# A split-precision decoder step on one core: float32 side work on every second unit, part of the weight splitting on GpSimd, a finer start and a spread convolution

## The chip, the core and the metric

The kernel runs on one core of one Trainium2 chip. The metric is the device time of one execution in microseconds (us). The kernel before takes 1319.54 us, the median of three runs that lie between 1318.51 and 1319.89.

The engines are named as the profile names them: PE is the matrix engine (PEld its weight loads), DVE the vector engine, ACT the scalar engine, POOL is GpSimd, SP the sync engine, which here only issues transfers. Each engine runs its own instructions strictly in the order in which the program issued them, and waits at an instruction until what it needs has been signalled.

## The reference, cut to what matters

One step of a one-layer decoder, in float32, for 256 prompt tokens and 8 x 8 sample tokens (320 columns in all) at a width of 2048:

```python
z = rmsnorm(x, g_mix) @ w_in                    # 2048 x 3584
b, c, hc, q, k, v, qx = jnp.split(z, IN_SPLITS, axis=-1)
# three head groups, side by side
y_conv = b * short_conv(c * hc, conv_w)         # width 512, 3 taps, 2 rows of history
y_swa  = sink_attention(q, k, v, rel_bias, ...) # 8 q heads, 2 kv heads, window 128
y_x    = cross_attention(qx, mk, mv)            # 4 heads, 256 memory tokens (w_mem_k, w_mem_v)
x = x + concat([y_conv, y_swa, y_x]) @ w_out
x = x + square(relu(rmsnorm(x, g_mlp) @ w_up)) @ w_down   # 2048 x 8192 and back
```

q, k and qx are normalized per head. Besides y, the new caches are returned (keys, values, memory keys and values, and the last rows of the convolution's input).

## The kernel before

**Tiling.** Activations are kept transposed, 128 channels by 320 columns per k-tile. All weights are float32. They come in 360 *pieces* of 256 rows by 512 columns (512 KB each), loaded by SP into four `raw` buffers. Each piece is split in two: ACT copies it to `wh`, rounded to the matrix engine's fast float32 format, and DVE forms `wl = raw - wh`, the rest (`split_piece`, L407). Activations are split the same way into S0h and S0l or S1h and S1l. A product is then three fast matmuls: wh by the high part, wh by the low part, wl by the high part. So there are 8256 main matmuls of 320 columns and 192 of 512 columns (those of the memory keys and values).

**Order of the work.** The pieces are taken in groups of 512 output columns: first seven groups of w_in with the two memory groups between (cross-attention q, then k and v, memory k, memory v, q, q, c, h, b), then w_out, then w_up and w_down in turns. A *unit* is 12 main matmuls (6 in the memory groups). The whole instruction order is written out by a planner while the program is built: `run_unit` (L469) issues a unit, `boundary` (L461) then steps the side jobs through `Side.step` (L218). A side job (norms, attention, bias, convolution) is a generator that issues some instructions, then yields for so many units. `after(tiles)` (L272) makes a job yield until a model of the engines' clocks (`Pace`, L98) says that the tiles are ready; `bank()` (L276) makes it yield until one of four PSUM banks is free. `side.until` (L237) steps jobs without issuing matmuls until named flags are up. What the planner writes is an order; waits on the chip happen where its model was wrong.

**The side work on PE.** Between units the jobs place *side visits*: transposes and attention scores in plain float32, others in the fast format, and the sample attention in column-tiled matmuls (32 output rows each). In the trace main matmuls write `mm` and all side visits write `ax`.

**Splitting.** `split_piece` for piece i+4 can start once piece i's unit is done. The function `rest` in it (L426) issues the subtraction on DVE and after it the load of the next piece on SP. POOL issues small transfers (table of the relative bias, the one-hot matrix c_hot, sinks, selector, g_k_x), six 128x512 memsets, and outputs.

**The convolution.** `h_evac` (L1124), called for each of four 128-row blocks m when its h is done, makes u = c*h, and at once the three taps: one `tensor_scalar` and two `scalar_tensor_tensor` on DVE over 336 columns. `b_evac` (L1153) multiplies by b.

**The start.** SP loads two k-tiles of x, the first piece in two halves, two more k-tiles of x, piece 1, four k-tiles of x in two loads, piece 2, and so on. ACT's queue loads the small columns table and the identity. Nine matmuls on ones keep PE busy until the first data land. In the first 48 main matmuls, the first two pieces go m pair by m pair: all matmuls of a piece for two blocks m, then for the other two.

**Lines to follow.** Nearly all instructions are recorded at one helper line, L166 (in the changed file L169), so groups are told apart by tile names.

Of the kernel before, what the change touches and what calls it, by code (L numbers as in the profile page):

```python
# [34 lines left out]
LAG = 6.0  # L35
WARM = 9
# [56 lines left out]
class Pace:  # L93
# [12 lines left out]
    def cost(self, eng, op, out, ins):  # L106
        n = max(a.free_size() for a in [out] + ins)
        if eng == "pe":
            n = out.free_size()
            if ins[0].dtype == F32R:  # L110
                return 0.0033 + n / 2400.0
            quarter = 0.25 if out.partition_size() == 32 else 1.0
            return 0.0009 * n if op == "transpose" else max(0.11, n / 600.0) * quarter
        if eng == "act":
            return 0.1 + n * 0.00083
        if eng == "dve":
            return 0.08 + n * 0.00104
# [17 lines left out]
    def load(self, out):  # L135
        start = max(self.clock["dma"], self.clock["pe"])
        self.clock["dma"] = start + out.free_size() * 4 * out.partition_size() / 330e3
        self.wrote[out.name] = (self.clock["dma"] + (2.0 if out.name.startswith("raw") else LAG), "dma")

# [7 lines left out]
class Paced:  # L147
# [3 lines left out]
    def __getattr__(self, op):  # L151
# [4 lines left out]
        def issue(*args, **kw):  # L156
            aps = [a for a in list(kw.values()) + list(args) if isinstance(a, bass.AP)]
            out = kw["out"] if "out" in kw else args[0]
            if op == "dma_start":
                if out.name not in self.pace.dram:  # L160
                    self.pace.load(out)
            else:
                if "accum_out" in kw:
                    self.pace.wrote[kw["accum_out"].name] = (self.pace.clock[self.name] + 0.5, self.name)
                self.pace.issue(self.name, op, out, [a for a in aps if a is not out])
            return f(*args, **kw)  # L166
# [81 lines left out]
def trunk_step(ctx: ExitStack, tc: tile.TileContext, I, O):  # L248
# [27 lines left out]
    def bank():  # L276
        return ax.need([P, 512])
# [20 lines left out]
    act.dma_start(out=ident, in_=I["c_ident"])  # L298
# [24 lines left out]
    rm = const.tile([P, 2], F32, name="rm")  # L323

# [71 lines left out]
    def load_piece():  # L396
# [3 lines left out]
        count["load"] += 1  # L400
        w, k0, c0 = pieces[i]
        t = raw_p.tile([P, 2, 512], F32, name="raw", tag="raw")
        for c in [slice(0, 2)] if i else [slice(0, 1), slice(1, 2)]:
            sp.dma_start(out=t[:, c, :], in_=w[c0 // 512, k0 // 2][:, c, :])
        wt[i] = t

    def split_piece():  # L407
# [9 lines left out]
        if not i:  # L417
            for c in range(2):
                side.until([f"x0{c}"])
                act.activation(out=h[:, c, :], in_=r[:, c, :], func=AF.Copy)  # L420
                dve.tensor_tensor(out=l[:, c, :], in0=r[:, c, :], in1=h[:, c, :].bitcast(F32), op=ALU.subtract)
            load_piece()
# [9 lines left out]
    def add_group(w, c0, korder, a, evac, kind="std", needs=None, pre=None, k0=0):  # L432
# [6 lines left out]
        if kind == "std":  # L439
            ends = [[([m], [i, i + 1]) for m in range(4)] for i in (0, n - 2)]  # L440
            if not base:
                ends[0] = [([2 * q, 2 * q + 1], [i]) for i in range(2) for q in range(2)]
# [26 lines left out]
    def run_unit(un):  # L469
# [10 lines left out]
        if un["kind"] == "std":  # L480
# [40 lines left out]
    def load_x(b, cuts=((0, 4),)):  # L521
        t = lx.must([P, 4, T])
        for lo, hi in cuts:
            sp.dma_start(out=t[:, lo:hi, :], in_=I["xT"][:, 4 * b + lo:4 * b + hi, :])
        xblk[b] = t
# [10 lines left out]
    def x_job():  # L536
        for i in range(8):
            for k in (2 * i, 2 * i + 1):
                split_act(S0h[:, k, :], S0l[:, k, :], xblk[k // 4][:, k % 4, :], gcol("g_mix", k))
                if not i:  # L540
                    side.flags.add(f"x0{k}")
                    yield 1
# [6 lines left out]
    def mean_rsqrt(out, sq):  # L549

        yield from after(sq)
        bk = yield from bank()
# [59 lines left out]
    def start_head(name, ps, gain, dest):  # L612
# [9 lines left out]
        def gen():  # L622
# [13 lines left out]
            bk = yield from bank()  # L636
# [146 lines left out]
    def cross_prompt(h):  # L783
# [4 lines left out]
        bk = yield from bank()  # L788
# [25 lines left out]
        bk = yield from bank()  # L814
# [24 lines left out]
    def cross_sample(f):  # L839
# [34 lines left out]
        for kb in range(2):  # L874
            t = yield from half()
            pool.memset(t, 0.0)
# [13 lines left out]
        for b in range(4):  # L890
            cur = queue.pop(0)
            yield from after(*cur)
            for kb in range(2):
# [38 lines left out]
    def swa_prompt(g, hp):  # L932
# [7 lines left out]
        for blk in range(2):  # L940
# [20 lines left out]
            yield 1  # L961
            pt = yield from half()
            act.activation(out=pt[:, 0:2 * nk], in_=bk[:, 0:2 * nk], func=AF.Copy)
            ax.put(bk)
            w2.put(s)
# [147 lines left out]
    def conv_pre_job():  # L1113
        st["u"] = yield from lx.need([P, 4, UC])
        cc = yield from half()
        pool.memset(st["u"][:, :, 0:2], 0.0)
# [250 lines left out]
```

## Time and profile before

| | us |
|---|---|
| median of three runs | 1319.54 |
| the profiled execution's own time | 1319.31 |
| its span (first to last instruction) | 1316.8 |
| what lies around the span | 2.5 |
| PE busy | 1309.4 (99%) |
| DVE busy | 675.2 (51%) |
| ACT busy | 540.5 (41%) |
| POOL busy | 17.7 (1%), 36 instructions |

The page counts PE as busy from the first modelled start of a matmul to its modelled end, so matmuls that follow each other overlap in it: one main matmul of 320 columns has a mean of 310 ns, while 12 of them in a row take 1.76 us in the chain of waits. So the pace is read from the chain, and durations of DVE, ACT and POOL instructions from the groups. A wait of PE is listed with the engine, or the transfer, whose signal ended it.

### The profile page before, as it was taken

To read this page: it belongs to the slowest core of one execution; us is meant where nothing else is said; L and a number is where in the kernel's file an instruction comes from. 1 tells how busy PE (TensorE), PEld (TensorE's weight loads), DVE (VectorE), ACT (ScalarE), POOL (GpSimd) and SP (SyncE) were. 2 spreads that over 40 slices of the span, in tenths; PEclk is the share of its full clock that TensorE was granted. 3 is DMA by queue.
4 is the path that set the end of the run, shared out by engine and by line. 5 is a ranking of instruction groups with operands and counts; after the bars stand their busy time and mean duration, and the time that the engine had idled before them with its cause. 6 is when DMAs were issued, how large, how long until landed. Compare 5 with 4: busy or idle time off the path is not lost.

```text
span 1316.8 us, 21550 instructions
## 1 busy us (share of the span) xinstructions
PE 1309.4 (99%) x8954; PEld 1286.9 (98%) x8954; DVE 675.2 (51%) x1022; ACT 540.5 (41%) x801; POOL 17.7 (1%) x36
## 2 busy tenths in 40 slices
PE   9999999999999999999999999999999999999998
PEld 8988999999999999999999999999999999999998
DVE  6876666776576444444344444344443344444342
ACT  7784554343355344332244432234442324433321
POOL 1011000000000000000000000000000000000000
PEclk9999999999999999999999999999999999999999
DMA  8667545366344444444444444444444444444552
GB/s 310 240 200 267 189 165 200 109 220 250 128 145 161 145 152 136 160 147 158 146 155 133 152 159 154 147 157 129 160 154 152 153 151 128 161 154 152 176 167 72
DMA packets 65025, 217.03 MB, mean 165 GB/s; under 512 B 8374, under 2 KB 10142, under 8 KB 64897
## 3 DMA queue, kind: packets, MB, share of 16 engines
q1 hardware_dynamic: 62896, 210.38, 47.8%
q0 software_dynamic: 1744, 5.19, 1.1%
q8 instruction: 70, 1.15, 0.4%
q14 instruction: 27, 0.21, 0.0%
q10 hardware_dynamic: 288, 0.10, 0.0%
HBM read 211.53 MB, written 7.65 MB: 166 GB/s over the span
## 4 chain that ended last, share of the span: by engine, by line
PE 98%; DMA 1%; DVE 0%; SPq 0%; ACT 0%; issue 0%; POOL 0%; DVEq 0%
PE mm L166 95%; PE ax L166 3%; DMA raw<-in_w_in 0%; DMA w<-in_c_hot 0%; DVE wl L166 0%; SPq L166 0%; ACT wh L166 0%; POOL z L166 0%; DVE lx L166 0%; DVE S0l L166 0%; DVEq L166 0%; DVE z L166 0%
## 5 line engine op out<-in xcount | busy, mean ns | idle before, releaser
L166 DVE TENSOR_TENSOR wl<-raw,wh 128x1024 fp32r<-128x1024 f32 (+1 forms) x361 | 435.9, 1220 | 479.8 <-ACT wh L166 473.2
L166 ACT ACTIVATE wh<-raw 128x1024 fp32r<-128x1024 f32 (+1 forms) x361 | 374.1, 1052 | 629.5 <-PE mm L166 591.0
L166 PE MATMUL mm<-S0h,wh 128*128 128x320 f32 x1472 | 458.1, 311 | 0.4 <-ACT wh L166 0.4
L166 PE MATMUL mm<-S0h,wl 128*128 128x320 f32 x1472 | 455.3, 309 | 1.6 <-DVE wl L166 1.6
L166 PE MATMUL mm<-S0l,wh 128*128 128x320 f32 x1472 | 454.8, 309 | 0.0
L166 PE MATMUL mm<-S1h,wh 128*128 128x320 f32 x1280 | 397.3, 310 | 0.0
L166 PE MATMUL mm<-S1h,wl 128*128 128x320 f32 x1280 | 395.5, 309 | 0.0
L166 PE MATMUL mm<-S1l,wh 128*128 128x320 f32 x1280 | 395.5, 309 | 0.0
L166 PEld LDWEIGHTS mm<-S0h,wh 128*128 128x128 f32 x1472 | 276.4, 188 | 3.8 <-issue 2.7
L166 PEld LDWEIGHTS mm<-S0h,wl 128*128 128x128 f32 x1472 | 276.3, 188 | 2.6 <-DVE wl L166 2.6
L166 PEld LDWEIGHTS mm<-S0l,wh 128*128 128x128 f32 x1472 | 276.5, 188 | 0.1
L166 PEld LDWEIGHTS mm<-S1h,wh 128*128 128x128 f32 x1280 | 240.3, 188 | 0.7 <-issue 0.6
L166 PEld LDWEIGHTS mm<-S1l,wh 128*128 128x128 f32 x1280 | 240.3, 188 | 0.1
L166 PEld LDWEIGHTS mm<-S1h,wl 128*128 128x128 f32 x1280 | 240.2, 188 | 0.0
L166 DVE TENSOR_TENSOR lx<-mm,lx 128x320 f32<-128x320 f32 x96 | 46.9, 489 | 78.7 <-PE mm L166 78.6
L166 ACT ACTIVATE z<-z 128x320 f32<-128x320 f32 (+1 forms) x118 | 54.9, 469 | 65.3 <-DVE z L166 64.2
L166 DVE TENSOR_TENSOR S1l<-z,S1h 128x320 fp32r<-128x320 f32 x68 | 33.4, 491 | 51.8 <-ACT S1h L166 51.8
L166 ACT ACTIVATE S1h<-z 128x320 fp32r<-128x320 f32 x68 | 32.1, 471 | 8.1 <-DVE z L166 6.1
L166 DVE SCALAR_TENSOR_TENSOR z<-mm,r2b 128x320 f32<-128x320 f32 x64 | 31.0, 484 | 0.0
L166 PE MATMUL mm<-wh,S1h 128*128 128x512 f32 x64 | 25.6, 400 | 0.0
L166 PE MATMUL mm<-wh,S1l 128*128 128x512 f32 x64 | 25.1, 392 | 0.0
L166 PE MATMUL mm<-wl,S1h 128*128 128x512 f32 x64 | 25.0, 391 | 0.0
(160 smaller groups left out, 431.2 us busy)
## 6 DMA issues: line engine op xcount, KB each, us to landing
raw<-in_w_up SPq DMA_DIRECT2D x128, 512.0 KB, 3.3
raw<-in_w_down SPq DMA_DIRECT2D x128, 512.0 KB, 3.3
raw<-in_w_in SPq DMA_DIRECT2D x55, 512.0 KB, 4.3
raw<-in_w_out SPq DMA_DIRECT2D x32, 512.0 KB, 3.5
raw<-in_w_mem_k SPq DMA_DIRECT2D x8, 512.0 KB, 4.5
raw<-in_w_mem_v SPq DMA_DIRECT2D x8, 512.0 KB, 3.4
w<-in_cmk SPq DMA_DIRECT2D x16, 256.0 KB, 5.3
w<-in_cmv SPq DMA_DIRECT2D x16, 256.0 KB, 5.2
```

Source lines behind the costliest of these rows:

```text
L166: return f(*args, **kw)
```

## The change

What the edits do:

1. **Float32 side visits on even units.** `bank()` now hands out a bank only at units with an even number; the fast-format visits ask with `bank(1)` and are placed at any unit. The two loops of the sample cross attention also wait for an even unit. The visits on PE become 60 instead of 70.
2. **Half of the early subtractions on POOL.** For pieces 8, 10, ... 102 (48 pieces) `wl = raw - wh` is issued on POOL instead of DVE, in the same place of the program. The memsets of the sample attention's probabilities and of the convolution's history columns go from POOL to DVE, and the transfer of the convolution's history goes from SP to POOL's queue.
3. **The start.** The first x k-tile is loaded on ACT's queue behind the columns table, the identity goes to POOL's queue, the first two pieces come in halves between the next k-tiles of x, and the first 48 matmuls go k-tile by k-tile: for each, four with wh and the high part (one for each m), four with wh and the low part, four with wl. The first k-tile's high part is made by DVE instead of ACT. One more warm-up matmul.
4. **The convolution spread.** `h_evac` makes u only. A new job, `conv_job`, makes the taps of one m every second unit; `b_evac` waits for its flag.
5. **Planner's numbers and the end.** Other constants in `Pace` (costs, a lag of 5 instead of 6 us for loads, twice that for loads on POOL's queue), other limits for jobs; the loads of the residual for w_out are spread over two groups; the last block's final addition and store go in two halves on ACT's and SP's queues.

On POOL, from its first transfer on, before (z takes the relative bias table, w_4 the one-hot matrix, w_5 and w_6 are the sample q of the cross attention, zeroed first, rv_d and sk_d are scratch in device memory):

```order
L166 DMA z_346<-in_rel_bias_table 32x8
L166 DMA w_4_347<-in_c_hot 33x384
L166 DMA skb<-in_sinks 128x8
L166 DMA sel<-in_c_sel 128x4
L166 DMA gkx<-in_g_k_x 128x128
L166 MEMSET w_5_435 128x512
L166 MEMSET w_6_436 128x512
L166 DMA rv_d<-w_11_486 8x384
L166 DMA sk_d<-rv_d 1024x1x384
L166 DMA z_1093<-sk_d 8x136 x8
```

and in the change, behind the identity's transfer:

```order
L169 DMA z_352<-in_rel_bias_table 32x8
L169 DMA w_4_353<-in_c_hot 33x384
L169 DMA skb<-in_sinks 128x8
L169 DMA sel<-in_c_sel 128x4
L169 DMA cc<-in_cconv 128x64
L169 DMA gkx<-in_g_k_x 128x128
L169 ISA
L169 TENSOR_TENSOR wl<-raw,wh 128x1024
L169 MEMSET w_5_445 128x512
L169 MEMSET w_6_446 128x512
L169 TENSOR_TENSOR wl<-raw,wh 128x1024
L169 DMA rv_d<-w_13_541 8x384
```

[...] Ahead of `rv_d` and `sk_d` stand the subtractions of pieces 8 and 10; the next ones follow behind.

On PE, the matmul that uses c_hot (tile w2_4, the first side visit; with the rows' tile numbers), before, where it stands behind 168 main matmuls:

```order
L166 MATMUL mm_187<-S0h_117,wh_340 128x320
L166 MATMUL mm_187<-S0l_118,wh_340 128x320
L166 MATMUL mm_187<-S0h_117,wl_341 128x320
L166 MATMUL ax_2_460<-w2_4_347,z_1_346 8x384 [waits DMASW1_49,DMASW0_49,DVE_49]
L166 MATMUL mm_204<-S0h_117,wh_300 128x320
```

and in the change, where it stands behind 192, at the seam from the first group to the second:

```order
L169 MATMUL mm_189<-S0l_118,wh_346 128x320
L169 MATMUL mm_189<-S0h_117,wl_347 128x320
L169 MATMUL ax_2_510<-w2_4_353,z_1_352 8x384 [waits DMASW2_49,DMASW1_49,DVE_49]
L169 MATMUL mm_522<-S0h_117,wh_388 128x320 [waits Activation_49]
L169 MATMUL mm_522<-S0l_118,wh_388 128x320
L169 MATMUL mm_522<-S0h_117,wl_389 128x320 [waits Pool_49]
```

wh_388 and wl_389 are the two parts of piece 8: the third main matmul behind the visit waits for POOL's first subtraction.

On DVE, where the last two blocks m of h are evacuated (lx is u, z the sum of the taps, `mm` the h of a block), before:

```order
L166 TENSOR_SCALAR z_2922<-lx_1375,cols 128x336
L166 SCALAR_TENSOR_TENSOR z_2922<-lx_1375,cols,z_2922 128x336 x2
L166 TENSOR_TENSOR z_2944<-mm,rb 128x320
L166 TENSOR_TENSOR lx_1375<-z_2944,lx_1375 128x256
L166 TENSOR_TENSOR lx_1375<-z_2944,lx_1375 128x8x8
L166 TENSOR_SCALAR z_2944<-lx_1375,cols 128x336
L166 SCALAR_TENSOR_TENSOR z_2944<-lx_1375,cols,z_2944 128x336 x2
L166 TENSOR_TENSOR wl<-raw,wh 128x1024
```

and in the change:

```order
L169 TENSOR_TENSOR z_2953<-mm,rb 128x320
L169 TENSOR_TENSOR lx_1381<-z_2953,lx_1381 128x256
L169 TENSOR_TENSOR lx_1381<-z_2953,lx_1381 128x8x8
L169 TENSOR_SCALAR z_2960<-lx_1381,cols 128x336
L169 SCALAR_TENSOR_TENSOR z_2960<-lx_1381,cols,z_2960 128x336 x2
L169 TENSOR_TENSOR wl<-raw,wh 128x1024
L169 TENSOR_SCALAR z_3000<-lx_1381,cols 128x336
L169 SCALAR_TENSOR_TENSOR z_3000<-lx_1381,cols,z_3000 128x336 x2
```

Only the first block's taps stand ahead of the subtraction now; the second block's follow behind it, the third's and fourth's later still.

The diff, cut to its core:

```diff
@@ Pace, Paced @@
-LAG = 6.0
-WARM = 9
+LAG = 5.0
+WARM = 10
+POOLED = 8, 104
-                return 0.0033 + n / 2400.0
+                return 0.0135 + n / 2400.0
-    def load(self, out):
+    def load(self, out, queue):
-        self.wrote[out.name] = (self.clock["dma"] + (2.0 if out.name.startswith("raw") else LAG), "dma")
+        self.wrote[out.name] = (self.clock["dma"] + (2.0 if out.name.startswith("raw") else 2 * LAG if queue == "pool" else LAG), "dma")
@@ bank @@
-    def bank():
-        return ax.need([P, 512])
+    def bank(every=2):
+        while side.now % every:
+            yield 1
+        t = ax.get([P, 512])
+        while t is None:
+            yield every
+            t = ax.get([P, 512])
+        return t
@@ split_piece @@
+        if i < 2:
             for c in range(2):
-                side.until([f"x0{c}"])
+                k = 2 * i + c
+                x = xblk[0][:, k, :]
+                if k:
+                    split_act(S0h[:, k, :], S0l[:, k, :], x, gcol("g_mix", k))
+                else:
+                    dve.tensor_scalar(out=S0h[:, k, :], in0=x, scalar1=gcol("g_mix", k), scalar2=None, op0=ALU.mult)
...
+        eng = pool if not i % 2 and POOLED[0] <= i < POOLED[1] else dve
         def rest():
-            dve.tensor_tensor(out=l, in0=r, in1=h.bitcast(F32), op=ALU.subtract)
+            eng.tensor_tensor(out=l, in0=r, in1=h.bitcast(F32), op=ALU.subtract)
             load_piece()
@@ run_unit @@
+        if len(un["ms"]) == 4:
...
+            for n, (w, x) in enumerate(((h, ah), (h, al), (l, ah))):
+                for m in un["ms"]:
+                    pe.matmul(out=grp[m][:, 0:T], lhsT=w[:, j, m * P:(m + 1) * P], rhs=x[:, k, :],
+                              start=u == 0 and n == 0, stop=False)
@@ cross_sample (both loops over b) @@
             yield from after(*cur)
+            while side.now % 2:
+                yield 1
@@ bias_job @@
+        pool.dma_start(out=ident, in_=I["c_ident"])
         pool.dma_start(out=bt[0:32, 0:8], in_=I["rel_bias_table"])
         pool.dma_start(out=hot[0:33, 0:384], in_=I["c_hot"])
         pool.dma_start(out=skb, in_=I["sinks"].to_broadcast([P, NH]))
         pool.dma_start(out=sel, in_=I["c_sel"])
+        pool.dma_start(out=cc, in_=I["cconv"].rearrange("p m r -> p (m r)"))
         pool.dma_start(out=gkx, in_=I["g_k_x"].to_broadcast([P, P]))
@@ convolution @@
-        dve.tensor_scalar(out=z, in0=u[:, m, 0:336], scalar1=gcol("conv_w", m), scalar2=None, op0=ALU.mult)
-        for i in (1, 2):
-            dve.scalar_tensor_tensor(out=z, in0=u[:, m, i:i + 336], scalar=gcol("conv_w", 4 * i + m), in1=z,
-                                     op0=ALU.mult, op1=ALU.add)
-        st["y"][m] = z
+        zs.put(z)
         if m == 3:
-            side.add("convout", conv_out_job())
+            side.add("convy", conv_job())
+    def conv_job():
+        u = st["u"]
+        for m in range(4):
+            z = yield from zt()
+            dve.tensor_scalar(out=z, in0=u[:, m, 0:336], scalar1=gcol("conv_w", m), scalar2=None, op0=ALU.mult)
+            for i in (1, 2):
+                dve.scalar_tensor_tensor(out=z, in0=u[:, m, i:i + 336], scalar=gcol("conv_w", 4 * i + m), in1=z,
+                                         op0=ALU.mult, op1=ALU.add)
+            st["y"][m] = z
+            yield 2
+        side.add("convout", conv_out_job())
@@ b_evac @@
-        side.until(["cp"])
+        side.until(["cp", "convy"])
@@ down_evac @@
+            if last and g == 3 and m == 3:
+                for queue, c in ((act, slice(0, T // 2)), (sp, slice(T // 2, T))):
+                    dve.tensor_tensor(out=a[:, c], in0=ps[:, c], in1=a[:, c], op=ALU.add)
+                    queue.dma_start(out=O["yT"][:, KT - 1, c], in_=a[:, c])
+                return
@@ the first loads @@
-    load_x(0, ((0, 2),))
+    load_x(0, 0, 1, act)
     load_piece()
-    sp.dma_start(out=xblk[0][:, 2:4, :], in_=I["xT"][:, 2:4, :])
     load_piece()
-    load_x(1, ((0, 2), (2, 4)))
+    for k in range(4):
+        if k:
+            load_x(0, k, k + 1, sp)
+        load_part(k // 2, slice(k % 2, k % 2 + 1))
+    load_x(1, 0, 2, sp)
     load_piece()
-    load_x(2)
+    load_x(1, 2, 4, sp)
     load_piece()
-    load_x(3)
+    load_x(2, 0, 4, sp)
+    load_x(3, 0, 4, sp)
```

More of the change, by code (lines that the diff above doesn't have):

```diff
@@ L323, in trunk_step @@
     rm = const.tile([P, 2], F32, name="rm")
+    cc = const.tile([P, 64], F32, name="cc")
     def gcol(name, i=0):
@@ L400, in load_piece, with load_part @@
         count["load"] += 1
+        wt[i] = raw_p.tile([P, 2, 512], F32, name="raw", tag="raw")
+        if i > 1:
+            load_part(i, slice(0, 2))
+    def load_part(i, c):
         w, k0, c0 = pieces[i]
[L402 to L405, printed above, removed]
+        sp.dma_start(out=wt[i][:, c, :], in_=w[c0 // 512, k0 // 2][:, c, :])
     def split_piece():
@@ L441, in add_group @@
             if not base:
-                ends[0] = [([2 * q, 2 * q + 1], [i]) for i in range(2) for q in range(2)]
+                ends[0] = [(list(range(4)), [i]) for i in range(2) for _ in range(2)]
             plan = ends[0] + [([2 * q, 2 * q + 1], [i]) for i in range(2, n - 2) for q in range(2)] + ends[1]
@@ L519, in trunk_step, with load_x @@
     xblk, mblk = {}, {}
[L521 to L525, printed above, removed]
+    def load_x(b, lo, hi, queue):
+        if b not in xblk:
+            xblk[b] = lx.must([P, 4, T])
+        queue.dma_start(out=xblk[b][:, lo:hi, :], in_=I["xT"][:, 4 * b + lo:4 * b + hi, :])
     def load_m(i):
@@ L536, in x_job @@
     def x_job():
-        for i in range(8):
+        for i in range(2, 8):
             for k in (2 * i, 2 * i + 1):
                 split_act(S0h[:, k, :], S0l[:, k, :], xblk[k // 4][:, k % 4, :], gcol("g_mix", k))
-                if not i:
-                    side.flags.add(f"x0{k}")
-                    yield 1
             side.flags.add(f"x{i}")
@@ L813, in cross_prompt @@
         yield from after(pt[1])
-        bk = yield from bank()
+        bk = yield from bank(1)
         for kb in range(2):
@@ L875, in cross_sample @@
             t = yield from half()
-            pool.memset(t, 0.0)
+            dve.memset(t, 0.0)
             pm.append(t)
@@ L892, in cross_sample @@
             yield from after(*cur)
+            while side.now % 2:
+                yield 1
             for kb in range(2):
@@ L1114, in conv_pre_job @@
         st["u"] = yield from lx.need([P, 4, UC])
-        cc = yield from half()
-        pool.memset(st["u"][:, :, 0:2], 0.0)
-        sp.dma_start(out=cc[:, 0:64], in_=I["cconv"].rearrange("p m r -> p (m r)"))
-        yield from after(cc)
+        dve.memset(st["u"][:, :, 0:2], 0.0)
         for m in range(4):
@@ L1304, in trunk_step @@
     side.add("cp", cross_prompt_all(), needs=xq + ["mk", "mix"], cost=2, heavy=1)
-    side.add("convpre", conv_pre_job(), needs=["rb", "mix"], cost=1)
+    side.add("convpre", conv_pre_job(), needs=["rb", "mix"])
     side.add("cs1", cross_sample(1), needs=xq + ["cs0"], cost=6, heavy=2)
@@ L1309, in trunk_step @@
         for i in range(2):
-            side.add(f"swp{g}{i}", swa_prompt(g, i), needs=qn + [f"k{g}", f"v{g}", "bias", "cp"], cost=3, heavy=1)
+            side.add(f"swp{g}{i}", swa_prompt(g, i), needs=qn + [f"k{g}", f"v{g}", "bias", "cp"], cost=2, heavy=1)
     for g in range(2):
@@ L1313, in trunk_step @@
         for i in range(2):
-            side.add(f"sws{g}{i}", swa_sample(i, g), needs=qn + [f"k{g}", f"v{g}", "biass", "cp"], cost=2, heavy=1)
+            side.add(f"sws{g}{i}", swa_sample(i, g), needs=qn + [f"k{g}", f"v{g}", "biass"], cost=2, heavy=1)
     split_piece()
-    side.until(["x1"])
     split_piece()
-    flush(subs)
     for un in units:
```

39 lines of the change are left out of this document (24 added, 15 removed).

## The prediction

> **What bounds the kernel now.** I read the page's busy times, its chain of waits, and the list of PE's waits.
>
> ```profile
> PE 1309.4 (99%) x8954; PEld 1286.9 (98%) x8954; DVE 675.2 (51%) x1022; ACT 540.5 (41%) x801; POOL 17.7 (1%) x36
> PE mm L166 95%; PE ax L166 3%; DMA raw<-in_w_in 0%; DMA w<-in_c_hot 0%; DVE wl L166 0%; SPq L166 0%; ACT wh L166 0%; POOL z L166 0%; DVE lx L166 0%; DVE S0l L166 0%; DVEq L166 0%; DVE z L166 0%
> PE mm L166 <- DVE wl L166: 1.6, 3, 1.1
> PE ax L166 <- DMA w<-in_c_hot: 0.8, 1, 0.8
> PE mm L166 <- ACT wh L166: 0.4, 1, 0.4
> ```
>
> The chain is PE's own queue for 98% of the span, and the change does not alter the number of main matmuls. So DVE time saved (the 48 subtractions) gains nothing by itself; it can only gain through one of the short waits listed: at the start, at c_hot, and the 1.1 us for wl. On the other side, any new wait of PE goes into the time in full. PE is the clock; I ask of each edit where PE will be waiting.
>
> **Part 1, even units.** Does a side visit cost PE anything beside its instructions? These pieces of the chain answer it:
>
> ```profile
> 116.88 1.76 PE mm L166 x12
> 143.53 0.11 PE ax L166
> 250.31 0.22 PE ax L166 x2
> 116.45 0.44 PE ax L166 x4
> 280.65 0.87 PE ax L166 x8
> 99.07 1.00 PE ax L166 x16
> 141.58 1.95 PE mm L166 x12
> ```
>
> Passes of 128 columns cost 0.11 each whether a visit has one, two, four or eight (0.11, 0.22, 0.44, 0.87), and the 12 main matmuls behind them take their usual 1.76. Joining such visits therefore saves nothing. Only behind the column-tiled visits (x16) do the 12 that follow take 1.95, about 0.2 more. The order shows about as many of these visits as before, 18 or 19. So 10 visits fewer is worth 0, between -0.4 (two such visits fewer, at 0.2) and +0.4 (a job that comes later makes its user wait). I take 0.
>
> **Part 3, the start.**
>
> ```profile
> 2.60 6.21 DMA raw<-in_w_in
> 8.83 1.07 ACT wh L166
> 9.92 1.24 DVE wl L166
> 11.21 14.06 PE mm L166 x94
> 5.67 0.57 PE L166 MATMUL mm<-S0h,wh 128*128 128x320 f32 x1 [0.40 <-ACT wh L166]
> 11.68 1.06 ACT L166 ACTIVATE wh<-raw 128x1024 fp32r<-128x1024 f32 x1 [1.79 <-DMA raw<-in_w_in]
> 1.21 0.42 ACTq L166 DMA_DIRECT2D ident<-in_c_ident  x1
> ident<-in_c_ident ACTq DMA_DIRECT2D x1, 64.0 KB, 4.0
> 12.78 1.23 DVE L166 TENSOR_TENSOR wl<-raw,wh 128x1024 fp32r<-128x1024 f32 x1 [1.63 <-ACT wh L166]
> 13.92 1.01 DVE L166 SCALAR_TENSOR_TENSOR S0l<-lx,cols,S0h 128x320 fp32r<-128x320 f32 x2
> ```
>
> PE begins at 5.67, does 26 main matmuls and waits for wl of piece 1 until 11.21. From there it runs at 1.76/12 = 0.147 each. Had it run so from the first, it would have begun at 11.21 - 26 x 0.147 = 7.39. That "zero" is what counts. In the change x's first k-tile stands where the identity stood on ACT's queue, issued at 1.2; with the identity's 4.0 us it lands at 5.2, its high part is made by about 5.8, and the first matmul starts about 5.9. Then each k-tile feeds 12 matmuls, 1.76 us, while halves of pieces arrive; the last half of piece 1 lands when piece 1 does now (8.81, the same bytes ahead of it), is split in about 1.3 and needed only after 36 matmuls, at 11.2. Piece 2 is needed at 5.9 + 48 x 0.147 = 12.95. It landed at 11.68, with all of x's third and fourth pair ahead; now half of that is behind it, so it lands about 0.8 earlier, 10.9, and its wl is done about 13.1; DVE makes the low part of k-tile 4 behind that, 0.5 more. PE waits about 0.75. Zero 6.65, a gain of 0.7; between -1.5 (no wait) and +0.3 (x's first k-tile later by 1.0, as behind a busy queue).
>
> **Parts 2 and 4, two waits that go.**
>
> ```profile
> 27.19 0.67 POOL z L166
> 27.85 5.09 DMA w<-in_c_hot
> 32.94 0.14 issue
> 33.07 0.80 PE ax L166 x2
> 259.46 0.05 DVEq L166
> 259.51 1.20 DVE wl L166
> 260.75 0.42 PE L166 MATMUL mm<-S0h,wl 128*128 128x320 f32 x1 [1.05 <-DVE wl L166]
> 258.38 1.18 DVE L166 SCALAR_TENSOR_TENSOR z<-lx,cols,z 128x336 f32<-128x336 f32 x2
> ```
>
> The bias matmul waits for c_hot until 33.07, 0.8 + 0.14 = 0.9 us. It now stands 24 main matmuls (3.5 us) later, less the 0.7 that PE is early: -0.9, bounds -0.9 and 0. At 259 the subtraction stood behind the fourth block's taps (1.18 and before that 0.4). With taps behind it and this piece, an even one, on POOL, the wait goes: -1.2 with the issue gaps, bounds -1.2 and 0. The last store in two halves: what follows the last matmul is one addition and one small store, either way; 0.
>
> **Part 2, the new wait.** This decides. When can POOL deliver piece 8's wl?
>
> ```profile
> 29.50 0.54 POOL L166 DMA_DIRECT2D gkx<-in_g_k_x  x1
> 30.03 1.01 POOL L166 MEMSET w<- 128x512 f32 x2
> 1.18 1.28 ACT L296 ACT_TABLE_LOAD   x1 [1.18 <-PEq L1354]
> z<-in_rel_bias_table POOLq DMA_DIRECT2D x1, 1.0 KB, 5.6
> 12.00:34.00 22.00, 21.22 (x142) 20.34 (x141) 17.74 (x24) 19.12 (x28) 3.86 (x7) 1.00 0.88 314
> ```
>
> POOL's transfers begin at 27.19, when DVE has set z; DVE's and ACT's chain up to there is tied to the landing of the first pieces and is the same now. [...] Then comes the subtraction itself. PE wants its result at 6.65 + 192 x 0.147 + 0.8 (bias) + 0.3 (two matmuls) = 35.95.
>
> The subtraction: no such operation of POOL is in the trace. A memset of 128x512 takes 0.5, so 1.0 for 1024 elements with one stream; three streams one after the other would take 3.0 to 3.4. Middle: 2.3. On DVE it takes 1.23.
>
> [...] A load of tables on ACT at an idle moment took 1.28; a transfer of 1 KB on POOL's queue, at this very place under a stream of 314 GB/s, took 5.6 to land. [...] POOL is done at 30.6 + 6.9 + 2.3 = 39.8, and PE waits 39.8 - 35.95 = 3.9. [...] Behind the waiting matmul stands all of PE's work; ACT and DVE get ahead meanwhile, so nothing more is late than piece 8. Piece 10 is wanted four units later (4 x 1.76 = 7.05 us), and POOL needs 1.0 + 2.3 for the two memsets and it; piece 12's subtraction stands behind two transfers that wait for the bias table, and has another 7.05. I take both as in time.
>
> [...]
>
> **Sum**, against the profiled 1319.31: -0.7 - 0.9 - 1.2 + 3.9 = +1.1, 1320.4. The median of the runs is 0.23 above the profiled one: 1320.6. For a few of 60 visits whose wl or operands come later, since POOL's 2.3 replaces 1.23, I add 0.3: **1320.9 us**.
>
> **Rivals.**
>
> [...]
>
> [...]
>
> *POOL holds DVE up* (slower, on top of my forecast).
>
> ```profile
> 66.00:120.00 54.00, 54.00 (x277) 43.12 (x276) 40.07 (x81) 37.19 (x79) 8.53 (x17) 1.00 0.70 237
> 120.00:232.00 112.00, 112.00 (x887) 107.97 (x886) 68.77 (x139) 55.68 (x104) 1.78 (x4) 1.00 0.57 191
> 232.00:353.00 121.00, 119.92 (x843) 114.60 (x842) 83.12 (x205) 46.20 (x107) 1.71 (x3) 1.00 0.50 177
> ```
>
> If DVE cannot read two operands while POOL reads, every subtraction on POOL stops DVE for up to 2.3 us. From 66 to 353 DVE is busy 40.07 + 68.77 + 83.12 = 192 of 287 us, 4.7 of each pair of pieces (7.05). Less 1.23, plus 2.3, it is 5.8: still no bound, but single visits come late by up to 2.3. If three do, by 1.2 on average, it is 3.6 more: 1324.5. Against it: DVE mostly waits for ACT there and has room.
> [...]
>
> *The change in PE's waits is nothing at all* (the subtractions are not late, but the start is no earlier and both waits reappear elsewhere): 1319.5, inside my forecast's range.
>
> **Chances.** Forecast (PE waits 2.5 to 5 us for piece 8; 1319.3 to 1322.5): 0.45. Load not felt: 0.25. Long load: 0.2. DVE held up: 0.1. The range of eight in ten: from 1316.2, the better start of the first rival, to 1326, between the two times of the long load. The forecast's own range is 1319.0 to 1322.5. Differences below 0.2% (2.6 us; 1316.9 and 1322.2) can't be told from no change. Of the load not felt, more than half is below 1316.9; the long load, the held DVE and the top of the forecast are above 1322.2: faster 0.2, same 0.43, slower 0.37.
>
> **What would show it.** In the profile after, PE's list of waits should name POOL wl with about 3.9 us, once, with PE idle from about 36 to 40; the POOL timeline should show a gap of about 7 between gkx and the first subtraction, and subtractions of about 2.3. The waits for c_hot and at 259 should be gone, and the 50th main matmul should run about 0.7 earlier. I am wrong if the gap is under 3 or over 8, or if DVE's mean time for two-operand instructions grows while POOL works.

## The result and the profile after

The change takes 1336.4 us (median; 1335.9 to 1337.17), beside 1319.69 us for the kernel before on the same chip: a ratio of 1.013, with an interval of 1.0117 to 1.0143. That is 16.7 us slower. Forecast were 1320.9 us, with a range up to 1326.

From the page of the change (span 1334.5 us): the busy times, POOL's slices, PE's granted clock, and the chain of waits by engine.

```profile
PE 1316.1 (99%) x8956; PEld 1289.2 (97%) x8956; DVE 685.6 (51%) x982; ACT 540.0 (40%) x801; POOL 133.8 (10%) x81
POOL 1343422232232000000000000000000000000000
PEclk9998999999999999999999999999999999999999
PE 90%; issue 3%; DVE 2%; ACT 1%; DMA 1%; POOL 1%; SPq 0%; DVEq 0%; POOLq 0%; ACTq 0%
```

PE was the chain for 98% of the span; now it is for 90%. POOL works in the first third alone, and in the same third, from 100 to 133 us, lies the only slice whose granted clock is below 0.9. DVE does 48 subtractions of 1.22 us fewer (58.7 us), but its busy time went up, from 675.2 to 685.6.

PE's waits in the change that matter here (us in total, times, longest):

```profile
PE ax L169 <- DMA w<-in_cmk: 5.3, 3, 3.4
PE mm L169 <- DVE z L169: 3.4, 1, 3.4
PE ax L169 <- DVE z L169: 3.4, 4, 1.4
PE mm L169 <- DVE S0l L169: 0.9, 1, 0.9
```

Nowhere does PE wait for POOL's `wl`. It waits for DVE's `z` and for the keys of the sample attention, `in_cmk`. By stretches (us; busy time and instructions of PE, its weight loads, DVE, ACT and POOL; granted clock, DMA share, GB/s), first before, then after:

```profile
66.00:136.00 70.00, 70.00 (x411) 58.72 (x410) 48.77 (x99) 42.80 (x85) 9.10 (x18) 1.00 0.71 240
```

```profile
66.00:136.00 70.00, 59.75 (x273) 45.28 (x272) 44.47 (x78) 41.75 (x88) 25.92 (x19) 0.93 0.53 184
```

PE was busy throughout; now it is idle for 10.25 of 70 us, and the clock is 0.93. The 411 instructions of before are now 273 in the same 70 us. Both stretches hold all 192 matmuls of 512 columns; of the main matmuls of 320 columns there are 25 instead of 119. From 136 to 360 us there is little to see: 222.91 busy before, 222.36 after.

The groups of DVE's instructions from 28 to 136 us (count, busy time, mean ns of one, idle time before them), before:

```profile
L166 DVE TENSOR_TENSOR wl<-raw,wh 128x1024 fp32r<-128x1024 f32 x32 | 39.0, 1223 | 25.2 <-ACT wh L166 22.3 <-DMA w<-in_cmk 2.8
L166 DVE SCALAR_TENSOR_TENSOR S1l<-w,cols,S1h 128x256 fp32r<-128x256 f32 x16 | 7.4, 479 | 0.6 <-ACT S1h L166 0.6
L166 DVE TENSOR_TENSOR z<-z,z 128x320 fp32r<-128x320 f32 x6 | 2.8, 485 | 0.0
L166 DVE SCALAR_TENSOR_TENSOR z<-ax,z 128x320 f32<-128x320 f32 x6 | 2.9, 484 | 0.0
```

and after:

```profile
L169 DVE TENSOR_TENSOR wl<-raw,wh 128x1024 fp32r<-128x1024 f32 x13 | 21.7, 1668 | 16.2 <-ACT wh L169 16.2
L169 DVE SCALAR_TENSOR_TENSOR S1l<-w,cols,S1h 128x256 fp32r<-128x256 f32 x16 | 14.1, 889 | 2.6 <-ACT S1h L169 2.6
L169 DVE TENSOR_TENSOR z<-z,z 128x320 fp32r<-128x320 f32 x6 | 4.9, 842 | 0.7 <-ACT z L169 0.7
L169 DVE SCALAR_TENSOR_TENSOR z<-ax,z 128x320 f32<-128x320 f32 x6 | 2.9, 484 | 0.0
```

The same instructions on the same shapes grew: the subtraction from 1223 to 1668 ns, `S1l` from 479 to 889, `z<-z,z` from 485 to 842. All three read their operands from SBUF. `z<-ax,z`, whose first operand `ax` is in PSUM, did not: 484 and 484.

How one of these becomes a wait of PE is in the timeline of the change (start, duration, engine; in brackets the idle time before and what ended it). The rows are put together from the views of POOL, DVE, ACT and PE, and rows between them are left out:

```profile
49.91 4.79 POOL L169 TENSOR_TENSOR wl<-raw,wh 128x1024 fp32r<-128x1024 f32 x2
49.72 6.07 DVE L169 TENSOR_TENSOR wl<-raw,wh 128x1024 fp32r<-128x1024 f32 x1 [0.47 <-ACT wh L169]
61.02 2.46 POOL L169 TENSOR_TENSOR wl<-raw,wh 128x1024 fp32r<-128x1024 f32 x1 [6.33 <-ACT wh L169]
61.13 2.90 DVE L169 TENSOR_TENSOR w<-w,w 128x512 f32<-128x512 f32 x1
63.96 0.87 DVE L169 SCALAR_TENSOR_TENSOR S1l<-w,cols,S1h 128x256 fp32r<-128x256 f32 x2
64.86 0.63 ACT L169 ACTIVATE w<-w 128x512 f32<-128x512 f32 x1 [3.52 <-DVE S1l L169]
67.07 0.89 ACT L169 ACTIVATE S1h<-w,cols 128x256 fp32r<-128x256 f32 x2
68.94 0.48 DVE L169 SCALAR_TENSOR_TENSOR S1l<-w,cols,S1h 128x256 fp32r<-128x256 f32 x1
69.34 0.48 DVE L169 TENSOR_TENSOR z<-mm,rb 128x320 f32<-128x320 f32 x1
69.97 0.71 PE L169 MATMUL mm<-wh,S1h 128*128 128x512 f32 x1 [3.42 <-DVE z L169]
70.48 0.63 PE L169 MATMUL mm<-wl,S1h 128*128 128x512 f32 x1
73.46 0.40 PE L169 MATMUL mm<-wh,S1l 128*128 128x512 f32 x1
```

DVE's `w<-w,w` takes 0.68 us in the trace before. Here it starts 0.11 after POOL's subtraction and ends 0.55 after POOL's end: 2.90. ACT, which had waited 3.52, goes on at 64.86, and DVE's `S1l` that needs ACT's `S1h` stands ahead of `z<-mm,rb`, which frees the PSUM bank that PE waits for, for 3.42 us. Then eight 512-column matmuls follow each other at 0.43 us (70.48 to 73.46 is seven of them), where later ones take 0.23.

On the chain that ends this wait stand the two stretched instructions, 6.07 us where such a subtraction takes 1.22, and 2.90 where 0.68 is usual: 7.1 us more, twice the wait. No transfer is on it.

The second long wait has another chain. POOL, SP and PE in the change, rows between left out:

```profile
105.91 2.41 POOL L169 TENSOR_TENSOR wl<-raw,wh 128x1024 fp32r<-128x1024 f32 x1 [3.24 <-ACT wh L169]
108.35 0.33 SPq L169 DMA_DIRECT2D raw<-in_w_in  x1
108.72 1.85 SPq L169 DMA_DIRECT2D w<-in_cmk  x4
112.70 1.07 PE L169 MATMUL ax<-w,w 128*32 128x256 f32 x4 [3.36 <-DMA w<-in_cmk]
```

SP waits with the load into a `raw` buffer until POOL has read it (105.91 + 2.41 = 108.32); the keys stand behind this load in SP's order, and PE waits 3.36 us for them. After this wait too the clock is low: 0.60 from 110 to 115 us and 0.72 from 115 to 120, beside 0.66 from 70 to 75 after the first. It is this second stretch that lies in the slice below 0.9.

### The profile page after: what moved, and what is told of

Same layout as the page of the kernel before. It is cut to its first block, busy times and chain, and to the rows that moved or that the text cites. A ratio compares the mean times of both kernels' runs of the same rounds, so it can differ in the third digit from the quotient of the medians.

```text
span 1334.5 us, 21557 instructions
## 1 busy us (share of the span) xinstructions
PE 1316.1 (99%) x8956; PEld 1289.2 (97%) x8956; DVE 685.6 (51%) x982; ACT 540.0 (40%) x801; POOL 133.8 (10%) x81
## 4 chain that ended last, share of the span: by engine, by line
PE 90%; issue 3%; DVE 2%; ACT 1%; DMA 1%; POOL 1%; SPq 0%; DVEq 0%; POOLq 0%; ACTq 0%
PE mm L169 87%; PE ax L169 3%; DMA raw<-in_w_in 1%; ACT wh L169 1%; POOL wl L169 1%; DVE w L169 0%; DVE z L169 0%; DVE wl L169 0%; DVE lx L169 0%; DVE S1l L169 0%; POOL z L169 0%; ACT lx L169 0%; DMA w<-in_cmv 0%; ACT S1h L169 0%; DVE S0l L169 0%
## 5 line engine op out<-in xcount | busy, mean ns | idle before, releaser
L169 DVE TENSOR_TENSOR wl<-raw,wh 128x1024 fp32r<-128x1024 f32 (+1 forms) x314 | 392.7, 1263 | 443.2 <-ACT wh L169 442.3
L169 POOL TENSOR_TENSOR wl<-raw,wh 128x1024 fp32r<-128x1024 f32 x48 | 117.3, 2446 | 242.0 <-ACT wh L169 232.9
L169 DVE TENSOR_TENSOR lx<-mm,lx 128x320 f32<-128x320 f32 (+1 forms) x97 | 46.9, 485 | 102.6 <-PE mm L169 95.6
```

## The experiments

Each row is the median in us, and the ratio to the kernel before as run beside it (1319.16 to 1319.69).

| kernel | us | ratio | interval |
|---|---|---|---|
| the change | 1336.4 | 1.0130 | 1.0117–1.0143 |
| e1: the 48 subtractions on DVE | 1324.98 | 1.0040 | 1.0026–1.0053 |
| e2: e1, POOL reads whole pieces | 1374.09 | 1.0414 | 1.0395–1.0433 |
| e3: e1, POOL only writes, twice | 1338.35 | 1.0143 | 1.0124–1.0161 |
| e4: before, with POOL subtractions | 1331.31 | 1.0089 | 1.0071–1.0108 |
| e5: e1, POOL only writes, once | 1334.57 | 1.0114 | 1.0084–1.0143 |
| e6: e1, POOL reads half a piece | 1358.08 | 1.0292 | 1.0262–1.0322 |
| e7: e1, load numbers of before | 1326.31 | 1.0048 | 1.0028–1.0068 |
| e8: e1, visits in every unit | 1320.20 | 1.0005 | 0.9994–1.0017 |
| e10: before, visits in even units | 1322.89 | 1.0028 | 1.0018–1.0038 |
| e12: e8, planner of before | 1319.16 | 0.9999 | 0.9990–1.0009 |
| e13: e1, POOL reads, holds no `raw` | 1357.24 | 1.0289 | 1.0268–1.0309 |
| e14: e13 with writes for reads | 1335.41 | 1.0123 | 1.0103–1.0144 |
| e15: no subtraction, POOL writes | 1329.47 | 1.0078 | 1.0060–1.0097 |
| e16: no subtraction, no POOL work | 1321.20 | 1.0015 | 1.0005–1.0026 |
| e17: before, two waits mended | 1318.79 | 0.9999 | 0.9990–1.0008 |

**Is it POOL, or the rest of the change?** e1 gives the subtractions back to DVE and leaves the order of every engine's work as the planner made it for POOL:

```diff
+    as_pool = Paced(pace, "pool", nc.vector)   # counted as POOL's, issued to DVE
-        eng = pool if not i % 2 and POOLED[0] <= i < POOLED[1] else dve
+        eng = as_pool if not i % 2 and POOLED[0] <= i < POOLED[1] else dve
```

> The changed kernel with every instruction in its place, but all 48 POOL subtractions run on DVE, at the same points of the program (the planner still counts them as POOL's, so the order on PE is the same to the row). Theory A (a POOL subtraction, which reads SBUF, stops every DVE instruction that takes its operands from SBUF until it ends, so the chains of DVE and ACT that feed PE come late): the time falls to about 1317.4 (1319.6 less 0.1 for the start as the trace of the change shows it, 0.9 for c_hot and 1.2 at the last block of h). Rival B (the new order itself, with its even units and later loads, makes the waits between 66 and 136 us): it stays at 1330 or more. Rival C (POOL only takes longer for a piece, 2.45 instead of 1.22 us, and keeps raw buffers longer): 1317, like A.

It took 1324.98: 11.4 of the 16.7 us are POOL's, and about 5.8 stay without it. DVE is busy for 676.4 us with the 48 subtractions, and for 622.3 in e16 (below), which leaves them out; in the change it was 685.6 without them. So its other instructions took some 63 us longer there.

e4 is the counterpart: the order of before, the subtractions on POOL.

```diff
+    as_dve = Paced(pace, "dve", nc.gpsimd)
+            eng = as_dve if not i % 2 and 8 <= i < 104 else dve
```

> The kernel before in its own order, with only one thing changed: the subtractions of pieces 8, 10, ... 102 run on POOL. Theory A: slower by 8 to 20 us, 1328 to 1340, with stretched DVE instructions between 30 and 360 us. Rival B (the new order is to blame): within 3 us of before, 1317 to 1323.

1331.31, 12 us above before: POOL's price does not come from the change's order. About 1.1 of the 12 lie at the start of the profiled execution, ahead of POOL's first subtraction, where the granted clock is 0.95 (from 0 to 34 us) instead of 1.00 before.

**What of POOL's work costs?** e2, e3, e5 and e6 add to e1, behind each of the 48 subtractions, an operation of POOL whose result nobody uses. e2 reads the whole of `wh` and writes the freed `raw` buffer, e3 sets that buffer twice, e5 once, e6 reads half a piece:

```diff
+            if eng is as_pool:
+                nc.gpsimd.tensor_tensor(out=r, in0=h.bitcast(F32), in1=h.bitcast(F32), op=ALU.subtract)   # e2
+                nc.gpsimd.memset(r, 0.0)                                                                  # e5; e3: twice
+                nc.gpsimd.tensor_tensor(out=r[:, 0, :], in0=h[:, 0, :].bitcast(F32), in1=h[:, 0, :].bitcast(F32), op=ALU.subtract)   # e6: half
```

> As e1_dve_sub, and behind each of the 48 subtractions that DVE makes again, POOL forms wh - wh into the raw buffer that DVE is done with, before the buffer is loaded again. No matmul waits for POOL; it only reads SBUF as long as in the change, about 2.4 us at a time. What it writes is never used. Theory A: DVE's instructions with operands in SBUF are stretched again and the time goes to 1330 to 1338. Rival C (PE waits for POOL's late result): 1317 to 1319, as nobody waits for POOL except the next load of that buffer.

> As e2_pool_reads, but POOL writes zeros into the raw buffer twice (2 x 1.05 us) instead of reading wh: POOL busy about as long, the buffer held about as long, the same order, but no reads by POOL. Theory A in its form 'only POOL's reads exclude DVE': 1317 to 1319, no stretched DVE instructions. If any work of POOL in SBUF stops DVE, or if the longer hold of raw buffers is what costs: 1328 or more, as e2_pool_reads.

> As e3_pool_sets, but POOL writes zeros into the raw buffer once (1.0 us) and not twice. The buffer is then free about 2.3 us after ACT's copy, much as in the change (2.45 us behind the copy), and POOL reads nothing. Theory A (reads stop DVE): 1325 to 1328, near e1_dve_sub. Theory H (what costs is that the next load of the buffer waits for POOL, and all of SP's queue behind it): 1331 to 1337, near the change.

> As e2_pool_reads, but POOL reads and writes half a piece (512 elements, about 1.25 us). The buffer is held as in e5_set_once within 0.3 us; the difference from e5_set_once is only that POOL reads. Theory A: 5 to 15 us above e5_set_once, with DVE instructions stretched by up to 1.2 us. Theory H: within 2 us of e5_set_once.

Reads cost: e2 is 35.7 us above e3, e6 23.5 above e5, at about the same time of POOL in each pair. But writes alone cost too: e5 is 9.6 us above e1 and e3 13.4, though DVE is busy for 678.9 and 681.0 us there, hardly more than e1's 676.4. This price stands in no step of the prediction. It shows at SP. PE's longest wait in e5:

```profile
PE mm L169 <- DVE z L169: 4.6, 1, 4.6
```

SP's transfers in e5 (duration is from the first's issue to the last's):

```profile
49.34 14.54 SPq L169 DMA_DIRECT2D raw<-in_w_mem_k  x3
63.97 0.38 SPq L169 DMA_DIRECT2D w<-in_mT  x1
```

and in e1:

```profile
48.14 3.60 SPq L169 DMA_DIRECT2D raw<-in_w_mem_k  x3
51.83 0.38 SPq L169 DMA_DIRECT2D w<-in_mT  x1
```

and in the change itself:

```profile
52.36 4.36 SPq L169 DMA_DIRECT2D raw<-in_w_mem_k  x3
56.81 0.38 SPq L169 DMA_DIRECT2D w<-in_mT  x1
```

A load into a `raw` buffer waits until all who use the buffer are through (in the change, above, POOL is through at 108.32 and the load goes out at 108.35); as long as they are not, they hold it. In e5 three loads take 14.54 us to be issued instead of 3.60. SP works in order, so the load of the next part of m, `in_mT`, which needs no `raw` buffer, comes at 63.97 instead of 51.83; ACT and DVE prepare that part late, and PE waits 4.6 us behind them for `z`. In the change the same three loads take 4.36 us and `in_mT` comes at 56.81: its wait for `z` is not this one. What holds SP in e5 is seen best in e15 (below).

**Reads without the hold.** e13 and its twin e14 let POOL write to a tile of its own (one tile taken from the pool of small ones), so that no `raw` buffer waits for it:

```diff
-    w2 = Slots(w2p, "w2", NW2)
+    w2 = Slots(w2p, "w2", NW2 - 1)
+    scratch = const.tile([P, 512], F32, name="scratch")
+                for c in range(2):                                                               # e13
+                    nc.gpsimd.tensor_tensor(out=scratch, in0=h[:, c, :].bitcast(F32), in1=h[:, c, :].bitcast(F32), op=ALU.subtract)
+                nc.gpsimd.tensor_copy(out=scratch[:, 0:1], in_=h[:, 0, 0:1].bitcast(F32))        # e14
+                for _ in range(4):
+                    nc.gpsimd.memset(scratch, 0.0)
```

> As e1_dve_sub, with DVE making all subtractions, and beside each of the 48 POOL forms wh - wh in two halves (2 x about 1.2 us) into a buffer that nothing else uses (one of twelve small tiles is given up for it, which moves one normalization visit). No raw buffer is held and nobody waits for POOL. Theory A (reads stop DVE): 8 to 25 us above e14_free_sets, with DVE stretched. If reads alone do no harm and only the held buffers did: within 2 us of e14_free_sets.

> The twin of e13_free_reads, instruction for instruction the same on PE, DVE, ACT and SP: POOL writes zeros into the unused buffer four times (4 x 0.5 us) in place of the reads. Theory A and theory H both: 1323 to 1327, near e1_dve_sub, since POOL neither reads nor holds a raw buffer.

The difference of the twins is clean: reads cost 21.8 us, near e6 against e5 (23.5). e14 against e1 is not, and it missed its expectation by 8 us. With one small tile fewer the planner moves ACT's and DVE's work (`rv_d` goes out at 64.80 instead of 43.79), so how much of e14's own 10.4 us is POOL cannot be said. Thus e13 and e14 do not show that the hold is what e5 pays for.

**The sum in the change's own order.** There POOL's work replaces DVE's instead of being added to it. e16 leaves the 48 subtractions out, on both engines, and PE takes `wh` in place of `wl` for those pieces (the result is then without these low parts). e15 does the same, and POOL sets the `raw` buffer twice, 2.0 us in all: meant as the hold without the reads.

```diff
-            eng.tensor_tensor(out=l, in0=r, in1=h.bitcast(F32), op=ALU.subtract)
+            if eng is pool:
+                pace.issue("pool", "tensor_tensor", l, [r, h.bitcast(F32)])   # counted, not issued
+                for _ in range(2):                                             # e15 alone
+                    nc.gpsimd.memset(r, 0.0)
+            else:
+                eng.tensor_tensor(out=l, in0=r, in1=h.bitcast(F32), op=ALU.subtract)
```

> The change in its own order on all engines, with the 48 subtractions left out altogether: the matmuls that take wl of these pieces take wh instead (same size), and POOL, where it subtracted, writes zeros into the raw buffer twice (2 x 1.0 us, once ACT's copy has read it). DVE is as unburdened as in the change, raw buffers are held until about 2.0 us after the copy (2.45 in the change), POOL reads nothing. Theory A (in the change the reads that stop DVE cost the 11 us): 1323 to 1327. Theory H (the held buffers do): 1332 to 1337, near the change. Both in part: between.

> As e15_left_out_held, but POOL does nothing for these pieces: neither hold nor reads, 48 subtractions less than e1_dve_sub for DVE. What an ideal helper would give: if DVE's time for the subtractions were worth anything to PE, clearly below e1_dve_sub (1325); by the prediction's first step (DVE time gains nothing by itself) 1323 to 1325.

e15 took 1329.47 and e16 1321.20. In e15 PE waits 3.9 us for the same `z` as in e5; in e16 that wait does not exist. The chain ahead of it in e15, from its second of the three loads on (start and duration; for a transfer, until it landed; short pieces left out):

```profile
53.25 6.92 DMA raw<-in_w_mem_k
60.25 1.07 ACT wh L171
61.35 1.24 DVE wl L171
62.60 0.33 SPq L171
63.02 3.72 DMA w<-in_mT
```

The third load, at 62.60, goes out when DVE has subtracted the very piece that the load before it brought. POOL was through with its own at 59.56. So the third load fills the buffer that the second has just filled. In the change, e1 and e16 the four `raw` buffers are taken in turn (in the change all three loads are out by 56.72, and the first of them lands after 59); in the runs in which POOL writes to `raw` (e2, e3, e5, e6, e15) they are not, as the semaphores that the loads wait for show. Why the buffers are handed out otherwise there was not followed. It means that e15, e5 and e3 hold SP in a way in which the change does not, and their prices are not the price of the change's hold.

So, with each engine's work in the same order: no subtractions 1321.2; on DVE (e1) +3.8, which holds DVE's time and the later release of the buffers together; on POOL +15.2, which is 11.4 more than on DVE. e15 lies between, 8.3 above e16 and 6.9 below the change, but these two numbers do not divide the 15.2 into hold and reads. What the traces show is that each came ahead of one of the change's two long waits of PE: DVE's stretched instructions ahead of the 3.42 us, POOL's hold of a buffer, and SP's order, ahead of the 3.36.

**The other 5.8 us.** e8 lets side visits into every unit again in e1; e10 puts the rule alone into the kernel before; e7 puts the planner's lag and rate of loads back in e1.

```diff
-    def bank(every=2):        # e8, on e1; e10 does the opposite, on before
+    def bank(every=1):
-            while side.now % 2:
-                yield 1
-LAG = 5.0                     # e7, on e1
+LAG = 6.0
-        self.clock["dma"] = start + out.free_size() * 4 * out.partition_size() / 410e3
+        self.clock["dma"] = start + out.free_size() * 4 * out.partition_size() / 330e3
```

> As e1_dve_sub, but the planner's numbers for loads are those of before: a lag of 6 instead of 5 us (12 on POOL's queue) and 330 instead of 410 bytes per ns. Nothing else; the planner then writes another order. Theory P (e1_dve_sub loses its 5.8 us because the planner believes that the sample attention's keys land sooner than they do, and PE waits for them at 101 and 110 us): 1317 to 1320, no waits for in_cmk. Rival E (the even-unit rule): 1324 to 1326.

> As e1_dve_sub, but without the rule of even units: bank() asks at every unit, and the sample attention's loops don't wait for an even one. 71 side visits instead of 60. Theory P: the waits for in_cmk stay, 1322 to 1326. Rival E (the rule pushes the sample attention and its loads together): 1317 to 1320.

> The kernel before with only the rule of even units added (59 side visits instead of 70, the planner's numbers as before). If the rule is what costs in itself (it bunches side jobs, and loads come later than their use): 1322 to 1326. If its cost in the change comes from its meeting the new numbers for loads: 1318.5 to 1320.5, as predicted for this part (0, between -0.4 and +0.4).

e7 stays at 1326.31: the load numbers are not it. e8 falls to 1320.2, 4.8 below e1, and e10 is 3.6 above before. The rule on even units costs 3.6 to 4.8 us. In e1 it is paid where a visit needs a load just issued. PE's first wait of the kind and SP's load in e1:

```profile
103.51 0.62 PE L169 MATMUL ax<-w,w 128*32 128x256 f32 x4 [1.75 <-DMA w<-in_cmk]
99.83 1.85 SPq L169 DMA_DIRECT2D w<-in_cmk  x4
```

before:

```profile
99.00 1.07 PE L166 MATMUL ax<-w,w 128*32 128x256 f32 x16
91.31 2.14 SPq L166 DMA_DIRECT2D w<-in_cmk  x4
```

Before, the keys were issued 7.7 us ahead of the matmuls and had landed; in e1 they are issued 1.9 us before PE wants them (103.51 - 1.75 - 99.83). Why SP comes to them 8.5 us later under the rule (in e8 it is at 91.33 again) was not followed further back. In the change the lead is 0.6 us and the longest wait 3.36, for POOL holds the load ahead of them. In e10 it shows otherwise: single waits of PE of 0.8 to 1.3 us for DVE and ACT, and none for `in_cmk`. That the rule costs some 4 us is common to both; through which waits depends on the order.

**Is there anything to be had?** e12 keeps from the change the new start, the visits for c_hot and the taps, and takes away POOL's work, the rule, and the planner's new numbers; e17 puts into the kernel before the early issue of c_hot and the taps behind the subtraction, nothing else.

```diff
-LAG = 5.0
+LAG = 6.0                                  # e12, with the other numbers of before
+        eng = dve
+    first_bias = zs.must([P, 336]), w2.must([P, 512])                             # e17, at the first loads
+    pool.dma_start(out=first_bias[0][0:32, 0:8], in_=I["rel_bias_table"])
+    pool.dma_start(out=first_bias[1][0:33, 0:384], in_=I["c_hot"])
+        subs.append(taps)                                                         # e17, in the convolution
```

> What is left of the change when the subtractions are DVE's, the rule of even units is gone and all of the planner's numbers are those of before: the finer start, the spread convolution, the shifted small transfers and the split last store. By the trace of e1_dve_sub the start gives 0.1 to 0.4, the later bias matmul 0.8 and the convolution 1.2: 1317.0 to 1317.5. If moved work turns up as new waits elsewhere: 1319 or more.

> The kernel before with two small edits in place of the change: the tile of the relative bias is set, and its transfer and c_hot's issued, at the program's start, and the taps of each block of h stand behind the subtraction that is due then. No rule of even units, no work on POOL, no finer start. If the two waits (0.9 and 1.2 us) go and nothing else moves: 1317.2. If the planner's other order gives back what they bring, as in e12_old_planner: 1319.

1319.16 and 1318.79: no difference from before that these runs can tell. In e12 the three old waits are gone, and PE's list has new, short ones in their place:

```profile
PE mm L169 <- DVE S1l L169: 0.7, 1, 0.7
PE ax L169 <- DVE S1l L169: 0.6, 1, 0.6
PE mm L169 <- DVE S0l L169: 0.5, 1, 0.5
PE ax L169 <- DVE w L169: 0.5, 1, 0.5
PE mm L169 <- DVE z L169: 0.4, 1, 0.4
```

2.7 us of new waits stand against 2.8 taken away. None of the kernels run here beats the one before by more than the runs scatter. The whole way, in medians: e12 1319.2, the planner's numbers +1.0 (e8; not to be told from none), the even units +4.8 (e1), POOL for DVE +11.4: 1336.4.

## Why the prediction was wrong

**"DVE time saved gains nothing by itself" (what bounds the kernel).** Off by up to 3.8 in the change's order: e16 against e1, where the buffers also come free earlier. That PE's list before named DVE with 1.6 us only does not say that DVE has room; its work from 66 to 136 us was 48.77 of 70.

**The new wait for piece 8 (+3.9, "this decides").** It did not come. POOL's timeline in the change:

```profile
30.54 0.54 POOL L169 DMA_DIRECT2D gkx<-in_g_k_x  x1
31.17 2.45 POOL L169 TENSOR_TENSOR wl<-raw,wh 128x1024 fp32r<-128x1024 f32 x1
```

The gap between the last transfer and the first subtraction is 0.09 us. No run shows the 6.9 that the sum has there; the row ISA, which stands between the two in the order, cost nothing that can be seen. Where the sum has 30.6, a time that no run shows either, POOL was through with its transfers at 31.08. The subtraction's own time was right, 2446 ns in the mean beside 2.3, and POOL was through, at 33.62, before PE's 35.95. Of that step the "load not felt" of the chances (0.25) had the truth, in that PE did not wait; its time failed with all the rest.

**The 0.3 for the other visits.** This is the step that failed. Behind piece 8 the prediction asked only whether POOL's results come in time for PE, and there they did. It measured +11.4. Of the signs of being wrong that it named, two came: a gap under 3 us, and a longer mean time of DVE's two-operand instructions. Two effects stand behind the 11.4; how they divide it is open.

- *The reads* were the rival "POOL holds DVE up", with chance 0.1 and 3.6 us. What it supposed is shown: by the groups above, with 479 to 889 ns for `S1l`, whose operands are in SBUF, and 484 unchanged for `z<-ax,z`, and by e13 against its twin that only writes (21.8 us where POOL's reads are added to DVE's work). The reason against it, "DVE mostly waits for ACT there and has room", was wrong: a DVE instruction of 0.48 us was held 2.9 longer (3425 ns at most), one of 1.22 that met two subtractions in a row took 6.07, and the chain from DVE to ACT to DVE to the PSUM bank passes such delays on to PE. "Up to 2.3 us" was too little for two in a row.
- *The hold* stood in no part. The prediction followed the buffer's readers forward to PE, and not back to the next load into it, nor to what stands behind that load on SP. The 0.3 counted POOL's 2.3 in place of 1.23 as a delay of a visit; at 108.35 us it was a delay of SP's whole in-order queue, with the keys in it. Its price in the change was not measured alone.

**Restart at a low clock.** The sum has no term for it. It came with the wait for `z`, and again with the wait of 3.36 us for `in_cmk` (granted clocks of 0.66 and 0.60, above). After the first, 3.42 us idle, PE's 512-column matmuls took 0.43 us for 3.4 us, then 0.23: 1.6 lost for eight.

**Part 1, even units (0, from -0.4 to +0.4).** Its own passes indeed cost nothing more (PE is busy for 1309.4 us in e10, as before). But +3.6 (e10) and +4.8 (e1 against e8) were measured. The upper bound, "a job that comes later makes its user wait", was the right mechanism, put at a tenth of its size: no row was looked up for how far ahead of their use the loads for the visits are issued (7.7 us for `in_cmk` before).

**Part 3, the start (-0.7).** With PE's rate of 0.147, the matmuls behind the first four k-tiles place the zero at 7.30 in the change, 6.99 in e1, 6.92 in e12 and 6.49 in e8, beside 7.49 before (7.39 at the matmul where the prediction took it): 0.2 gained in the change, up to 1.0 elsewhere. PE's timeline in the change:

```profile
14.38 0.42 PE L169 MATMUL mm<-S0l,wh 128*128 128x320 f32 x1 [0.85 <-DVE S0l L169]
```

The wait for the low part of k-tile 4 came nearly as foreseen, 0.85 for 0.75. Why the change gains less here than the others was not traced.

**Parts 2 and 4 (-0.9 and -1.2).** Right in their place: the visit with c_hot costs 0.94 us from the matmul before to the one behind, 1.78 before, so 0.84; the wait at 259 us is gone. But e12 and e17 show that the time does not follow: both keep these gains and end within 0.2% of before. In e12 new waits on late operands took their place; in e17 it was not traced what did. The sum added the gains as if they were independent, and the prediction's rival "no change in waits" (both reappear elsewhere) was right on these.

**The range** ended at 1326 because it was made from the one wait for piece 8; its two ends are that wait left out (1316.2) and a longer one, and no run shows the longer one. The other 47 subtractions were in it with 0.3.

## What to carry to other kernels

When an operation moves to another engine, follow each of its buffers backward too: who loads it next, in which in-order queue, and what stands behind that load; here PE never waited for a result of POOL's, but 3.36 us for keys that stood behind such a load, beside 1.75 with the subtractions on DVE. Ask what the busy engine's own instructions do while the helper reads SBUF: here DVE instructions with both operands in SBUF stretched by nearly the helper's whole duration (0.68 to 2.90 us beside an operation of 2.46), and work that is "only" moved off an engine at 50 to 75% can leave it busier (685.6 us with 48 instructions fewer). And a list of PE's waits that sums to 3 us is no budget to be won back: removing three of them gave 0 here, and bunching the side visits lost 4 us in waits for loads and operands that had been just early enough.

## What was not expected of the hardware

The first subtraction on POOL started 0.09 us after the transfer ahead of it, where the sum has 6.9; in e14 POOL's first copy started as the transfer ahead of it ended (at 30.73, beside 30.20 + 0.56).

POOL's side was stretched too, on as little as a copy of a single column. Two of these copies in e14:

```profile
40.81 1.17 POOL L454 COPY scratch<-wh 128x1 f32<-128x1 f32 x1 [6.08 <-ACT wh L169]
55.79 0.18 POOL L454 COPY scratch<-wh 128x1 f32<-128x1 f32 x1 [1.85 <-ACT wh L169]
```

It took 1.17 us where a DVE subtraction was running (from 40.71 to 41.93) and 0.18 where none was. POOL's memsets, 2 us for each of 48 pieces, left DVE's times where they were: in e3, from 28 to 75 us, 1.21 to 1.23 us for each subtraction and 0.48 for each `S1l`.

What stays open: how POOL's 11.4 us in the change divide between the reads and the held buffers, why the loads take other buffers once POOL writes to `raw`, and how much POOL's reads alone would cost where they replace DVE's work; the 21.8 us were measured where DVE did all the subtractions as well. That DVE's own wide subtractions are then among the instructions held up fits a higher price, but no run took them apart.
